# The last 64 rows of a down-projection: two full-height products per bank replaced by three half-height products on the two halves of TensorE's rows

## The chip, the cores and the metric

The kernel is one layer of a hybrid decoder (attention part, gated MLP, final norm) in float32 for 2048 tokens of width 1024. It runs on one core of a Trainium2 chip. The metric is the device time of one execution in microseconds (us). Three runs of the kernel before gave 3138.59, 3139.66 and 3145.38 us; the median is 3139.66 us.

## The reference, cut to what matters

Only the very end of the layer is touched: the down-projection of the gated MLP, the gated residual add and the final norm.

```python
D_MODEL = 1024; SEQ = 2048
D_FF = int(round(8 * D_MODEL / 3 / 64)) * 64        # 2752 = 21 * 128 + 64
...
    u = causal_depthwise_conv(h @ w_up[l], conv_w[l], conv_b[l])
    u_gate, u_val = jnp.split(u, 2, axis=-1)
    x = x + gate_m * ((jax.nn.silu(u_gate) * u_val) @ w_down[l])
return rms_norm(x, g_final)
```

The contraction runs over 2752 rows of `w_down`, which is 21 blocks of 128 and one of 64.

## The kernel before, in words

Matrix products are made in TensorE's one-pass float32 type. To keep float32 precision every operand is held in two parts, high and low: `split` (line 43) rounds the operand on ScalarE (line 44, `hi`), and another engine subtracts that from the operand (line 45, `lo`). A product of two such operands is then three products into the same bank of PSUM, high by high, high by low and low by high; low by low is left out.

The down-projection (lines 926 to 993) runs over four blocks of 512 tokens (`tb`). A block has eight banks of PSUM, four groups `t` of 128 tokens by two halves `n` of the 1024 output columns. In the names of the profile the banks of `t` = 0 and 1 are `ps_o`, those of `t` = 2 are `ps_t`, those of `t` = 3 are `ps_bc`. For each block `k` of contraction rows, `load` (line 928) brings 128 rows of `w_down` (`wdraw`) and of the activations (`graw`) from DRAM and splits them into `wd` and `g`: ScalarE makes both high parts, VectorE the low part of `wd`, GpSimd the low part of `g`. The buffers of `wd` and `g` are six each. `step` (line 957) issues the three products of one `k`, one `t` and one `n`. Each has a weight load of 128x128 from `g` and streams 512 columns of `wd`.

For `k` = 0 to 17 the products of all eight banks are issued `k` by `k` (lines 964 to 971). The last four, `k` = 18 to 21, are kept in `tail` and issued bank by bank (lines 972 to 981), so that a bank is finished, multiplied by the gate (line 983), added to the residual (line 984) and squared (line 986) while TensorE goes on with the next one. After both halves of a group `t`, its norm is made (lines 987 to 989) and the result scaled and written out (lines 992 and 993).

The block `k` = 21 has 64 rows only, and is loaded twice, to partitions 0 to 63 and 64 to 127. In `wd` both copies are split alike. In `g` the upper copy is the high part (line 941) and the lower copy is replaced by the low part (line 942), so that one product over 128 rows gives high plus low of the activations by one part of the weights. Two such products, with `wd` high and `wd` low, make this block: two for each bank, four for each `t`. This also adds low by low, at no further instruction.

The kernel is written in straight code and a scheduler sets the order in which each engine's instructions stand, from the code and from its own estimate of times; the engines wait for one another by semaphores, each engine in its own order. A line elsewhere is of use below: the transposes of line 537 take four blocks of 43 rows through TensorE, in the attention part. The built program gives every product a tile of TensorE's rows and columns. Nearly all have the full 128x128 at row 0; these four have 64x128 at row 0.

Of the kernel before, what the change touches and what calls it, by code (L numbers as in the profile page):

```python
# [11 lines left out]
AF = mybir.ActivationFunctionType  # L12
# [4 lines left out]
P = 128  # L17
# [6 lines left out]
TB = 512  # L24
NTB = S // TB
DFF = 2752
NFULL = DFF // P
REST = DFF - NFULL * P
# [5 lines left out]
def kernel(ctx: ExitStack, tc: tile.TileContext, x, c, w_ada, b_ada, g_attn, w_in, b_fgate,  # L34
                      g_out_fox, g_out_sb, w_out, g_mlp, w_up, conv_w, conv_b, w_down, g_final, out):
    nc = tc.nc
# [3 lines left out]
    def f(t):  # L40
        return t.bitcast(F32)

    def split(hi, lo, src, lo_engine=None):
        nc.scalar.activation(hi, src, AF.Copy)  # L44
        (lo_engine or nc.gpsimd).tensor_sub(lo, src, f(hi))  # L45
# [52 lines left out]
    def modulate(pool, pst, xts, mod, dest, done, tag, lo_engine=None, affine_dve=False, junk=None, prepare=None):  # L98
        n = len(xts) * P
        step = 1 if prepare else len(xts)  # L100
        for j in range(0, len(xts), step):
            r = rms_scale(pool, xts[j:j + step], tag, junk)
            for i, xt in enumerate(xts[j:j + step]):
                nc.vector.tensor_scalar_mul(xt, xt, r[:, i:i + 1])
        yield
        hs_ = []
        for kt in range(KT):
            if prepare:
                prepare(kt)
            ps = pst()  # L110
            for i, xt in enumerate(xts):
                nc.tensor.transpose(ps[:, i * P:(i + 1) * P], xt[:, kt * P:(kt + 1) * P], ident)
            hf = pool.tile([P, n], F32, name=f"hf_{tag}", bufs=2)
            if affine_dve:
                nc.vector.tensor_scalar(hf, ps[:, :n], mod[:, 0, kt:kt + 1], mod[:, 1, kt:kt + 1], ALU.mult, ALU.add)
            else:
                nc.scalar.activation(hf, ps[:, :n], AF.Identity, scale=mod[:, 0, kt:kt + 1], bias=mod[:, 1, kt:kt + 1])
            h = dest(kt)
            split(h[:, 0], h[:, 1], hf, lo_engine)
            hs_.append(h)  # L120
            if kt:
                done(kt - 1, hs_[kt - 1])
            yield
        done(KT - 1, hs_[-1])
        yield
# [36 lines left out]
    def bank(pool, tag, bufs):  # L162
        return pool.tile([P, 512], F32, name=f"ps_{tag}", tag=tag, bufs=bufs)
# [20 lines left out]
    b = pv()  # L184
# [65 lines left out]
    def load_w(kind, p):  # L250
        base = (0 if kind == "fox" else 3 * 512) + p * P
        lo_engine = nc.vector if kind == "sb" else None

        def load(tag, kt, first, step):
            raw = sl_.tile([P, 2, P], F32, name=f"raw_{tag}", tag="wraw", bufs=3)
            nc.sync.dma_start(raw, w_in[kt * P:(kt + 1) * P, first:first + (step + 1) * P].rearrange(
                "p (a n) -> p a n", n=P)[:, 0:step + 1:step, :])
            n = 2 * P + (NH if tag == "v" else 0)
            w_ = sl_.tile([P, 2, n], F32R, name=f"w_{tag}", bufs=8)
            w = w_[:, :, 0:2 * P].rearrange("p s (a n) -> p s a n", n=P)  # L260
            split(w[:, 0], w[:, 1], raw, lo_engine)
            if tag == "v" and (kind, p) == ("sb", 0):
                split(w_[:, 0, 2 * P:], w_[:, 1, 2 * P:], wfr[:, kt], nc.vector)
            return w if tag == "qk" else w_

        def load_qk(kt):
            qk_.append(load("qk", kt, base, 4))

        def load_v():
            return [load("v", kt, base + 1024, 1) for kt in range(KT)] if p % 2 == 0 else None  # L270

        qk_ = []
        if (kind, p) == ("sb", 0):
            return [qk_, load_qk, load_v]
        for kt in range(KT):
            load_qk(kt)
        return [qk_, load_v()]
# [381 lines left out]
    for i, u in enumerate(units):  # L659
# [14 lines left out]
        if kind == "fox":  # L674
            n = sum(2 * (2 + 2 * tb + j2 + 1) for j2 in range(2)) + 1
        else:
            n = sum(2 * (tb + 1 + 2 * tb + j2 + 1) for j2 in range(2)) + 1
# [64 lines left out]
    def bank_a():  # L742
        return bank(psd, "o", 4)
# [139 lines left out]
    for sblk in range(2):  # L883
# [21 lines left out]
        a, b = bank_a(), bank_a()  # L905
# [22 lines left out]
    def load(k, tb):  # L928
        n = P if k < NFULL else REST
        g = dp.tile([P, 2, TB], F32R, name="g", bufs=6)  # L930
        wraw = dp.tile([P, D], F32, name="wdraw", bufs=3)
        graw = dp.tile([P, TB], F32, name="graw", bufs=2)
        w = dp.tile([P, 2, D], F32R, name="wd", bufs=6)
        for r in range(P // n):
            nc.sync.dma_start(wraw[r * n:(r + 1) * n], w_down[k * P:k * P + n, :])
            nc.sync.dma_start(graw[r * n:(r + 1) * n], gs[k][tb // 2][:, tb % 2 * TB:(tb % 2 + 1) * TB])
        split(w[:, 0], w[:, 1], wraw, nc.vector)
        if n == P:
            split(g[:, 0], g[:, 1], graw)
        else:  # L940
            nc.scalar.activation(g[:, 0], graw, AF.Copy)
            nc.vector.tensor_sub(g[REST:P, 0], graw[REST:P], f(g[REST:P, 0]))
        return g, w

    de = open_pool("end")
# [3 lines left out]
    NKD = NFULL + 1  # L949
    for tb in range(NTB):  # L950
        if tb == 0:
            nc.sync.dma_start(gm, gate_m)
            nc.sync.dma_start(gf, g_final.rearrange("(o n) -> o n", o=1).to_broadcast([P, D]))
        banks = [[bank(psd, "o", 4) for _ in range(2)] for _ in range(2)]
        banks += [[bank(psd, "t", 2) for _ in range(2)], [bank(psc, "bc", 2) for _ in range(2)]]

        def step(k, g, w, t, n):
            seq = ((0, 0), (0, 1), (1, 0)) if k < NFULL else ((0, 0), (0, 1))
            for i, (a, b) in enumerate(seq):
                nc.tensor.matmul(banks[t][n], g[:, a, t * P:(t + 1) * P], w[:, b, n * TB:(n + 1) * TB],  # L960
                                 start=k == 0 and i == 0, stop=k == NKD - 1 and i == len(seq) - 1)

        tail = []
        for k in range(NKD):
            g, w = load(k, tb)
            if k >= NKD - LAST:
                tail.append((k, g, w))
                continue
            for t in range(4):
                for n in range(2):  # L970
                    step(k, g, w, t, n)
        for t in range(4):
            row = tb * 4 + t
            xt = de.tile([P, D], F32, name="xo", bufs=4)
            nc.sync.dma_start(xt, x1s[row])
            ss = de.tile([P, 2], F32, name="sl_f", bufs=4)
            r = de.tile([P, 1], F32, name="r_f", bufs=4)
            for n in range(2):
                sl = slice(n * TB, (n + 1) * TB)
                for k, g, w in tail:  # L980
                    step(k, g, w, t, n)
                y = de.tile([P, TB], F32, name="yo", bufs=4)
                nc.vector.tensor_mul(y, banks[t][n], gm[:, sl])
                nc.vector.tensor_add(xt[:, sl], xt[:, sl], y)
                junk = de.tile([P, TB], BF16, name="junk_f", bufs=2)
                nc.scalar.activation(junk, xt[:, sl], AF.Square, accum_out=ss[:, n:n + 1])
            nc.vector.tensor_add(r, ss[:, 0:1], ss[:, 1:2])
            nc.scalar.activation(r, r, AF.Sqrt, bias=epsc, scale=1.0 / D)
            nc.vector.reciprocal(r, r)
            for n, q in enumerate((nc.sync, nc.scalar)):  # L990
                sl = slice(n * TB, (n + 1) * TB)
                nc.vector.scalar_tensor_tensor(xt[:, sl], xt[:, sl], r, gf[:, sl], ALU.mult, ALU.mult)
                q.dma_start(out[row * P:(row + 1) * P, sl], xt[:, sl])
# [27 lines left out]
```

## Time and profile before

| | |
|---|---|
| median of three runs | 3139.66 us |
| the profiled execution's own time | 3141.04 us |
| its span, first to last instruction | 3139.3 us |
| mean granted TensorE clock over the span | 0.983 |
| TensorE busy with products / with weight loads | 95% / 80% of the span |
| VectorE / ScalarE / GpSimd busy | 68% / 54% / 39% |
| first down-projection product starts | 2657.3 us |
| products of the down-projection (line 960) | 2080 |

The profile is of one execution. The time outside its span is 1.7 us. In the views a row of PE is a product, a row of PEld a weight load; a row with xN merges N instructions of a kind that follow one another, from the start of the first to the end of the last. Ends of products are modelled and overlap the next product, so distances between starts tell the rate.

### The profile page before, as it was taken

How to read it: one execution, taken by the hardware profiler on the slowest of the kernel's cores; microseconds unless marked ns; L12 is line 12 of the kernel's file. 1: busy time of each engine (PE TensorE's matmuls, PEld its weight loads, DVE VectorE, ACT ScalarE, POOL GpSimd, SP SyncE). 2: the span in 40 equal slices, each digit the busy share in tenths (PEclk: the TensorE clock that was granted, in tenths of full speed). 3: DMA queues.
4: the chain of work that ended last, by engine and by line, in shares of the span. 5: the costliest groups of instructions: out<-in, count | busy, mean ns of one | idle time of the engine just before them, and what ended most of it. 6: DMA issues, size and time to landing. Idle time of an engine off the chain costs nothing. (4 is left out here: it accounts for less than half of the span.)

```text
span 3139.3 us, 46425 instructions
## 1 busy us (share of the span) xinstructions
PE 2967.0 (95%) x15934; PEld 2511.6 (80%) x15934; DVE 2145.5 (68%) x3342; ACT 1691.0 (54%) x3161; POOL 1227.1 (39%) x1387
## 2 busy tenths in 40 slices
PE   6889998989989999999999999999899998999998
PEld 5778787877878889888877678888678887888887
DVE  6787888878875876556843587778987776354253
ACT  5666776666756676567744444444444444343332
POOL 1554455456553242242212344344444442322321
PEclk8999999999999999999999999999999999999999
DMA  9547542555336696585446632222222223554552
GB/s 267 177 140 255 168 136 69 182 185 155 123 108 221 214 314 211 158 313 162 164 158 222 212 97 86 86 83 83 82 82 89 85 81 130 190 199 161 189 199 90
DMA packets 292940, 496.51 MB, mean 158 GB/s; under 512 B 29448, under 2 KB 177664, under 8 KB 291680
## 3 DMA queue, kind: packets, MB, share of 16 engines
q1 hardware_dynamic: 281072, 480.92, 47.9%
q10 hardware_dynamic: 11632, 12.63, 1.1%
q8 instruction: 126, 2.06, 0.3%
q14 instruction: 110, 0.90, 0.1%
HBM read 352.61 MB, written 90.51 MB: 141 GB/s over the span
## 5 line engine op out<-in xcount | busy, mean ns | idle before, releaser
L810 PE MATMUL ps_o<-oa,wu 128*128 128x512 f32 x2088 | 503.5, 392 | 14.4 <-DVE oa L45 6.9
L810 PEld LDWEIGHTS ps_o<-oa,wu 128*128 128x128 f32 x2088 | 390.5, 188 | 105.5 <-DVE oa L45 10.7
L397 PE MATMUL ps_pv<-at,V 128*128 128x256 f32 x2304 | 410.9, 296 | 41.6 <-DVE at L393 24.8
L393 DVE TENSOR_TENSOR at<-ps_pt,at 128x512 fp32r<-128x512 f32 (+1 forms) x576 | 366.0, 653 | 102.8 <-ACT at L392 99.8
L281 PE MATMUL ps_pj<-hp,w_qk 128*128 128x512 f32 x1512 | 418.4, 406 | 11.1 <-ACT hp L44 3.1
L420 POOL TENSOR_TENSOR a<-a,r 128x512 f32<-128x512 f32 (+3 forms) x240 | 283.4, 1182 | 368.8 <-DVE r L416 112.3
L392 ACT ACTIVATE at<-ps_pt 128x512 fp32r<-128x512 f32 (+1 forms) x576 | 319.4, 577 | 179.8 <-PE ps_pt L388 147.3
L397 PEld LDWEIGHTS ps_pv<-at,V 128*128 128x128 f32 x2304 | 337.0, 192 | 84.6 <-DVE at L393 42.8
L281 PEld LDWEIGHTS ps_pj<-hp,w_qk 128*128 128x128 f32 x1512 | 275.7, 191 | 65.4 <-POOL hp L45 4.0
L45 DVE TENSOR_TENSOR wd<-wdraw,wd 128x1024 fp32r<-128x1024 f32 x88 | 112.4, 1277 | 261.4 <-ACT wd L44 261.4
L378 PE MATMUL ps_qk<-K,Q 128*128 128x512 f32 (+2 forms) x640 | 264.1, 414 | 11.3 <-DMA K<-q 5.8
L419 DVE TENSOR_TENSOR_SCAN r<-r 128x513 f32<-128x513 f32 x192 | 258.0, 1355 | 21.7 <-ACT r L410 14.5
L45 POOL TENSOR_TENSOR g<-graw,g 128x512 fp32r<-128x512 f32 x84 | 141.3, 1684 | 326.8 <-ACT g L44 326.8
L960 PE MATMUL ps_o<-wd,g 128*128 128x512 f32 x1040 | 250.8, 391 | 8.8 <-ACT g L44 8.8
L810 PE MATMUL ps_t<-ob,wu 128*128 128x512 f32 x984 | 243.2, 392 | 0.0
L320 PE MATMUL ps_pj<-w_v,hp 128*128 128x256 f32 (+1 forms) x1536 | 234.1, 291 | 4.8 <-DVE q L45 2.2
L379 PE MATMUL ps_qk<-K,Q 128*128 128x512 f32 (+2 forms) x640 | 238.1, 373 | 0.0
L960 PEld LDWEIGHTS ps_o<-wd,g 128*128 128x128 f32 x1040 | 196.2, 189 | 50.0 <-ACT g L44 9.2
L44 ACT ACTIVATE wu<-wuraw 128x512 fp32r<-128x512 f32 x214 | 133.2, 626 | 185.5 <-PE ps_o L810 111.5
L320 PEld LDWEIGHTS ps_pj<-w_v,hp 128*128 128x128 f32 x1536 | 211.8, 193 | 15.5 <-DVE q L45 3.1
L810 PEld LDWEIGHTS ps_t<-ob,wu 128*128 128x128 f32 x984 | 186.2, 189 | 39.4 <-DVE wu L45 0.3
L388 PE MATMUL ps_pt<-edge,a 128*128 128x128 f32 x1088 | 187.3, 281 | 27.6 <-POOL a L420 14.7
(217 smaller groups left out, 5743.3 us busy)
## 6 DMA issues: line engine op xcount, KB each, us to landing
hp<-hs SPq DMA_DIRECT2D x224, 512.0 KB
wuraw<-in_w_up_dram SPq DMA_DIRECT2D x84, 512.0 KB
wdraw<-in_w_down_dram SPq DMA_DIRECT2D x84, 512.0 KB
Q<-q SPq DMA_DIRECT2D x128, 256.0 KB
g<-u SPq DMA_DIRECT2D x42, 512.0 KB
graw<-g SPq DMA_DIRECT2D x84, 256.0 KB
hs<-hp SPq DMA_DIRECT2D x32, 512.0 KB
K<-q SPq DMA_DIRECT2D x128, 128.0 KB
```

What stands on the lines that cost most here:

```text
L45: (lo_engine or nc.gpsimd).tensor_sub(lo, src, f(hi))
L281: nc.tensor.matmul(acc, w[kt][:, a, n], h[:, bb], start=kt == 0 and i == 0, stop=kt == KT - 1 and i == 2)
L320: nc.tensor.matmul(av[:, t * width:(t + 1) * width], hts[kt][:, a, tok], w[1][kt][:, bb, 0:width], start=kt == 0 and m == 0, stop=kt == KT ...
L378: nc.tensor.matmul(b[:, :cw], Q[:, hl, 0, qcols], K[:, hl, :cw], start=True, stop=False)
L379: nc.tensor.matmul(b[:, :cw], Q[:, hl, 1, qcols], K[:, hl, :cw], start=False, stop=True)
L392: nc.scalar.activation(at[:, 0, lo:], b[:, lo:], AF.Copy)
L393: nc.vector.tensor_sub(at[:, 1, lo:], b[:, lo:], f(at[:, 0, lo:]))
L397: nc.tensor.matmul(o[:, 0:2 * P], V[kt // 4][:, kt % 4, hl, :], rhs, start=first and kk == 0 and w == 0, stop=last and kk == 1 and w == 1)
L419: nc.vector.tensor_tensor_scan(rev, rev, rev, 1.0, ALU.mult, ALU.bypass)
L420: (nc.vector if (ch + qi) % 4 == 0 else nc.gpsimd).tensor_mul(a[:, :need], a[:, :need], r[:, 1:need + 1])
L810: nc.tensor.matmul(b, w[:, p, j], o[:, q], start=first and i == 0, stop=last and i == 2, skip_group_check=True)
L960: nc.tensor.matmul(banks[t][n], g[:, a, t * P:(t + 1) * P], w[:, b, n * TB:(n + 1) * TB], start=k == 0 and i == 0, stop=k == NKD - 1 and i ...
```

## The change

The 64-row block is taken out of `tail`. Its activations are now split as all others are: both copies of `g` get a high and a low part, the low part on GpSimd. A new function, `step_rest`, issues the three products high by high, high by low and low by high for each half `n` of the columns with a contraction of 64 rows: for `n` = 0 from partitions 0 to 63 and for `n` = 1 from partitions 64 to 127, in turns. It is called once for each `t`, ahead of the products of `k` = 18 to 20, and starts or stops no bank.

```diff
             nc.sync.dma_start(graw[r * n:(r + 1) * n], gs[k][tb // 2][:, tb % 2 * TB:(tb % 2 + 1) * TB])
         split(w[:, 0], w[:, 1], wraw, nc.vector)
-        if n == P:
-            split(g[:, 0], g[:, 1], graw)
-        else:
-            nc.scalar.activation(g[:, 0], graw, AF.Copy)
-            nc.vector.tensor_sub(g[REST:P, 0], graw[REST:P], f(g[REST:P, 0]))
+        split(g[:, 0], g[:, 1], graw)
         return g, w
...
         def step(k, g, w, t, n):
-            seq = ((0, 0), (0, 1), (1, 0)) if k < NFULL else ((0, 0), (0, 1))
-            for i, (a, b) in enumerate(seq):
+            for i, (a, b) in enumerate(((0, 0), (0, 1), (1, 0))):
                 nc.tensor.matmul(banks[t][n], g[:, a, t * P:(t + 1) * P], w[:, b, n * TB:(n + 1) * TB],
-                                 start=k == 0 and i == 0, stop=k == NKD - 1 and i == len(seq) - 1)
+                                 start=k == 0 and i == 0, stop=k == NFULL - 1 and i == 2)
+
+        def step_rest(g, w, t):
+
+            for a, b in ((0, 0), (0, 1), (1, 0)):
+                for n in range(2):
+                    r = slice(n * REST, (n + 1) * REST)
+                    nc.tensor.matmul(banks[t][n], g[r, a, t * P:(t + 1) * P], w[r, b, n * TB:(n + 1) * TB],
+                                     start=False, stop=False)
 
         tail = []
         for k in range(NKD):
             g, w = load(k, tb)
+            if k == NFULL:
+                rest = g, w
+                continue
             if k >= NKD - LAST:
...
             r = de.tile([P, 1], F32, name="r_f", bufs=4)
+            step_rest(*rest, t)
             for n in range(2):
```

The built program gives the products of `step_rest` tiles of 64x128, at row 0 for `n` = 0 and at row 64 for `n` = 1. Up to the down-projection every engine's instructions stand as before.

On TensorE the products stand as follows at the end of the last block of tokens, before the change. The last three rows are the tail: eleven products for each of the eight banks.

```order
L960 MATMUL ps_o<-wd,g 128x512 x12
L960 MATMUL ps_t<-wd,g 128x512 x6
L960 MATMUL ps_bc<-wd,g 128x512 x6
L960 MATMUL ps_o<-wd,g 128x512 x44
L960 MATMUL ps_t<-wd,g 128x512 x22
L960 MATMUL ps_bc<-wd,g 128x512 x22
```

At the same place after the change (line 955 is `step`, line 963 `step_rest`; the size is that of the output) this stands.

```order
L955 MATMUL ps_o<-wd,g 128x512 x12
L955 MATMUL ps_t<-wd,g 128x512 x6
L955 MATMUL ps_bc<-wd,g 128x512 x6
L963 MATMUL ps_o<-wd,g 128x512 x6
L955 MATMUL ps_o<-wd,g 128x512 x18
L963 MATMUL ps_o<-wd,g 128x512 x6
L955 MATMUL ps_o<-wd,g 128x512 x18
L963 MATMUL ps_t<-wd,g 128x512 x6
L955 MATMUL ps_t<-wd,g 128x512 x18
L963 MATMUL ps_bc<-wd,g 128x512 x6
L955 MATMUL ps_bc<-wd,g 128x512 x18
```

Each group `t` now begins with six products of half height, and the bank of its first half is finished nine products before that of its second half, where it was eleven.

On VectorE the program's last instructions stand so before: `yo` is a bank times the gate, `xo` the residual row, `r_f` the norm.

```order
L983 TENSOR_TENSOR yo<-ps_bc,gm 128x512
L987 TENSOR_TENSOR r_f<-sl_f 128x1
L984 TENSOR_TENSOR xo<-xo,yo 128x512
L989 RECIPROCAL r_f<-r_f 128x1
L992 SCALAR_TENSOR_TENSOR xo<-xo,r_f,gf 128x512 x2
L983 TENSOR_TENSOR yo<-ps_bc,gm 128x512
L984 TENSOR_TENSOR xo<-xo,yo 128x512
L987 TENSOR_TENSOR r_f<-sl_f 128x1
L989 RECIPROCAL r_f<-r_f 128x1
L992 SCALAR_TENSOR_TENSOR xo<-xo,r_f,gf 128x512 x2
```

After the change they stand so.

```order
L994 TENSOR_TENSOR r_f<-sl_f 128x1
L990 TENSOR_TENSOR yo<-ps_bc,gm 128x512
L996 RECIPROCAL r_f<-r_f 128x1
L991 TENSOR_TENSOR xo<-xo,yo 128x512
L999 SCALAR_TENSOR_TENSOR xo<-xo,r_f,gf 128x512 x2
L990 TENSOR_TENSOR yo<-ps_bc,gm 128x512
L991 TENSOR_TENSOR xo<-xo,yo 128x512
L994 TENSOR_TENSOR r_f<-sl_f 128x1
L996 RECIPROCAL r_f<-r_f 128x1
L999 SCALAR_TENSOR_TENSOR xo<-xo,r_f,gf 128x512 x2
```

Only the sum of the norm of `t` = 2 has moved, ahead of the first half's multiplication; the two scalings of `t` = 2 still stand between the two halves of `t` = 3.

## Rows read from the trace of the kernel before

**Rows 1.** The page: busy us of each engine, share of the span, instructions.
```profile
PE 2967.0 (95%) x15934; PEld 2511.6 (80%) x15934; DVE 2145.5 (68%) x3342; ACT 1691.0 (54%) x3161; POOL 1227.1 (39%) x1387
```

**Rows 2.** Busy us by stretch (PE, PEld, DVE, ACT, POOL), granted clock, DMA share, GB/s.
```profile
2774.00:2891.00 117.00, 117.00 (x518) 96.89 (x517) 47.65 (x55) 41.32 (x64) 35.59 (x21) 1.00 0.55 184
2891.00:3009.00 118.00, 118.00 (x522) 97.69 (x522) 48.53 (x57) 41.32 (x64) 35.30 (x21) 1.00 0.55 183
...
3111.15:3131.10 19.95, 19.95 (x89) 16.33 (x87) 13.43 (x26) 5.95 (x17) 0.00 (x0) 1.00 0.15 54
```

**Rows 3.** Waits, 2656 to 3140 us: us in total, times, longest.
```profile
POOL g L45 <- ACT g L44: 326.8, 81, 26.9
...
ACT wd L44 <- PE ps_bc L960: 196.8, 58, 3.9
...
PE ps_o L960 <- ACT g L44: 8.8, 1, 8.8
```

**Rows 4.** Chain that ended last, its last bank: start us, us, what.
```profile
3126.27 2.51 PE ps_bc L960 x11
...
3128.80 0.16 DVE yo L983
...
3130.33 1.42 DVE xo L992 x2
3131.74 0.61 DVE yo L983
```

**Rows 5.** TensorE's timeline, tail of the first block: start us, us, merged instructions.
```profile
2757.55 10.14 PE L960 MATMUL ps_o<-wd,g 128*128 128x512 f32 x44
2767.52 5.15 PE L960 MATMUL ps_t<-wd,g 128*128 128x512 f32 x22
...
2777.50 2.88 PE L960 MATMUL ps_o<-wd,g 128*128 128x512 f32 x12
...
2788.38 2.88 PE L960 MATMUL ps_o<-wd,g 128*128 128x512 f32 x12
```

**Rows 6.** TensorE's timeline in the attention part, around line 537.
```profile
946.40 0.39 PE L379 MATMUL ps_qk<-K,Q 128*128 128x512 f32 x1
946.63 0.60 PE L388 MATMUL ps_pt<-edge,p 128*128 128x128 f32 x4
947.16 0.44 PE L537 MATMUL ps_pt<-edge,hp 43*128 43x43 f32 x4
947.53 0.38 PE L378 MATMUL ps_qk<-K,Q 128*128 128x256 f32 x1
947.75 0.28 PE L379 MATMUL ps_qk<-K,Q 128*128 128x256 f32 x1
```

**Rows 7.** The same place in narrower stretches: products from 946.955, then from 947.36 us.
```profile
946.74 0.49 PE L388 MATMUL ps_pt<-edge,p 128*128 128x128 f32 x3
...
947.87 0.40 PE L281 MATMUL ps_pj<-hp,w_qk 128*128 128x512 f32 x1
```

**Rows 8.** All engines there, the loads and the VectorE work ahead of them.
```profile
946.54 0.16 DVE L490 SCALAR_TENSOR_TENSOR ls<-ls 128x4 f32<-128x4 f32 x1
...
947.16 0.32 PEld L537 LDWEIGHTS ps_pt<-edge,hp 43*128 43x128 f32 x4 [0.17 <-issue]
...
947.53 0.19 PEld L378 LDWEIGHTS ps_qk<-K,Q 128*128 128x128 f32 x1
```

**Rows 9.** Line 537's products: duration ns min/median/max.
```profile
L537 PE MATMUL ps_pt<-edge,hp x4: 232/232/253, 947.2 to 947.4; 43*128 43x43 f32 x4
```

**Rows 10.** All engines while the 64-row block of the first token block is split.
```profile
2747.84 0.61 ACT L941 ACTIVATE g<-graw 128x512 fp32r<-128x512 f32 x1
...
2749.22 0.69 DVE L942 TENSOR_TENSOR g<-graw,g 64x512 fp32r<-64x512 f32 x1
...
2753.97 1.80 POOL L45 TENSOR_TENSOR g<-graw,g 128x512 fp32r<-128x512 f32 x1 [9.07 <-ACT g L44]
```

**Rows 11.** ScalarE, where the next block takes over the tail's buffers.
```profile
2775.88 1.06 ACT L44 ACTIVATE wd<-wdraw 128x1024 fp32r<-128x1024 f32 x1 [0.58 <-PE ps_bc L960]
```

## The prediction, made before the change was run

> **What bounds the kernel now.** I read the page first: TensorE is busy for 95% of the span [rows 1], which says nothing yet about the stage that is changed. So I read busy time by stretch. In the two middle token blocks of the down-projection TensorE's busy time equals the stretch, 117.00 of 117.00 and 118.00 of 118.00 us, at a granted clock of 1.00, which is the 2.4 GHz level; the other four engines are busy for less than half of it [rows 2]. The list of waits agrees: in the whole stage TensorE waits once, 8.8 us at its very start, while GpSimd and ScalarE spend their time waiting for others [rows 3]. The chain that ended last runs through TensorE's products until 3128.78 us and leaves it only for the last bank's eviction [rows 4]. So a product taken out of this stage, or added, counts in full, and the price of one is the distance of starts: 9.97 us for 44 [rows 5], 0.2267 us. The recorded durations are longer and mean nothing here.
>
> The last 10.5 us deserve a look of their own. The second half of the last group is done on TensorE at about 3131.3 us (22 products after 3126.27), but its multiplication by the gate starts late, because VectorE is still scaling the rows of the group before: the chain goes from the first half's bank (11 products) by way of VectorE [rows 4]. The end hangs on when the *first* half of the last group is finished.
>
> **What goes.** 16 groups (four blocks, four `t`) lose four full-height products each: 4 × 0.2267 = 0.907 us a group. The subtraction on VectorE, 0.69 us in each block [rows 10], goes too; VectorE is not late in mid-stage, so that is worth nothing.
>
> **What comes, off the path.** GpSimd gets four subtractions of 1.80 us [rows 10], one a block. GpSimd is busy for 35 of 118 us [rows 2]. The high part of the block was written from 2747.84 us on; 0.61 and 1.80 us later, at about 2750.3, the low part can be there, and the tail starts at 2757.55 [rows 5]: over 7 us of cover. That the 64-row block is now used first in the tail and not last eats 2.0 us (9 products) which are not needed. If the cover were gone, a wait of up to 1.8 us a block would stand on TensorE, 7 us in all. The tail's buffers of `k` = 18 to 20 come free two products later in relation to the block's end (0.45 us). ScalarE now refills the first of them at 2775.88 [rows 11], and TensorE needs it only two steps into the next block, at 2788.38 [rows 5]: 11 us of cover, no cost.
>
> **What comes, on the path.** Each group gets six products over 64 rows, three pairs of an upper and a lower one.
>
> *The pairs.* No row shows two products on different halves of TensorE's rows. The bounds are full overlap, where a pair takes as long as one product, 3 × 0.227 = 0.68 us, and none, 6 × 0.227 = 1.36 us. I take full overlap. The nearest row for it is that of line 537, where the array is run as tiles of 64 rows: four products start 0.07 us apart ((0.44 − 0.23) / 3) although each lasts 0.23 us [rows 6, 9]. So in that mode several products are under way at once and the loads run ahead of them. The lower product must start after the upper one; after the last pair this lag stays: between 0 and 0.11 us (a full-height start, rows 6); I take 0.06, near line 537's distance.
>
> The Trainium skill (TensorE: Matmul & The Clock Gate, Part 3, measured speedup) says that products on different row groups run together, with starts some 4 ns apart, and gives 3.07 times for four of 32 rows. By that the lag would be nil and the sum below smaller by 1 us; no run here shows it yet.
>
> *Going into the 64-row mode.* The four transposes of line 388 ahead of line 537 start 0.11 us apart (946.63, 946.74), so the last starts at 946.96 [rows 6, 7]. The first load of line 537 starts 0.20 us later, at 947.16, together with its product, and its idle time is put down to "issue": nothing that it waited for; the last VectorE instruction that had ended by then did so 0.46 us before, at 946.70 [rows 8]. That is 0.09 us over the usual 0.11. Besides, the load is no longer hidden behind a running product. Between 0.02 us (longest against median product of line 537, rows 9) and 0.10 us (below); I take 0.10, since the new loads are of the same kind as those below and not transposes. Sum 0.19; lower bound 0, if the drain belongs to transposes alone.
>
> *Coming out of it.* The last product of line 537 starts at 947.16 + 0.44 − 0.23 = 947.37; the next load and product, full height again, start at 947.53, 0.16 later where 0.07 was the rule: 0.09 [rows 6, 8]. That product then lasts 0.38 us where its twin lasts 0.28, and the twin starts 0.22 us after it, where the next distance is 0.12 [rows 6, 7]: 0.10 us for a load that nothing hides. Sum 0.19; lower bound again 0.
>
> The Trainium skill has a rule that speaks against this change (TensorEngine Tiling (Array Packing), key properties): tiles run in parallel, but changing the tiling mode, not merely the tile, drains TensorE. The trace agrees, at 0.09 us each way plus a bare load; without that rule the sum would be the gain of the last rival below.
>
> *The sum.* A group: 0.19 + 0.68 + 0.06 + 0.19 − 0.91 = +0.21 us. Sixteen groups: +3.4 us.
>
> *The end.* The first half of the last group is now finished after the six and nine more products, and only nine follow it where eleven did. VectorE's work between the two halves is as long as before (3128.80 to 3131.74 us, rows 4), so the last eviction falls 2 × 0.227 = 0.45 us further behind TensorE: +0.4 us. Bounds: nothing, if VectorE keeps up, to 0.5.
>
> In total +3.8 us: the profiled execution's 3141.04 us would become 3144.8; that execution was 1.4 us above the median of the runs, 3139.66, so I predict 3139.66 + 3.8 = **3143.5 us**. By the bounds above it ends between 3141.2 (bare first load 0.02, no lag) and 3144.4 (lag 0.11).
>
> **The rivals.**
>
> *No overlap* (slower, the other side). If the lower product starts only when the upper one is through, a group takes 0.19 + 1.36 + 0.19 − 0.91 = +0.83 us, sixteen 13.3, with the end 13.8: 3153.4 us. For it: no row shows overlap of two halves. Against: the split of the array that rows 6 show by their drains would then serve nothing, and line 537's products overlap one another. It decides against the kernel as soon as a pair takes longer than about 0.29 us: 0.38 + 3 × 0.29 + 0.06 − 0.91 = +0.4, sixteen 6.4 us, which is 0.2%.
>
> *Overlap, but bare loads.* If the loads of one half don't run ahead while the other half works, each pair takes 0.227 + 0.10 = 0.33 us: a group 0.09 + 0.99 + 0.06 + 0.19 − 0.91 = +0.42, in total 6.7 + 0.4 = +7.1: 3146.8 us. Against it: line 537's loads do run ahead.
>
> *Free switching* (a small gain). If the drains of line 537 come from its being a transpose, or are covered behind products of 512 columns, a group takes 0.68 + 0.06 − 0.91 = −0.17, in total −2.7 + 0.4 = −2.3: 3137.4 us; at the very best 3136.5 (no lag, 16 × −0.227 = −3.6, end +0.4). For it: there is only one place in the trace to read the price from. Against: the row names no cause but issue, and the full-height transposes of line 388 follow a product without a break, 946.63 after 946.40 [rows 6].
>
> **How the numbers follow.** A difference under 0.2%, 6.3 us, is about what a measurement of this kernel can't tell from no change. Chances: mode switches at line 537's price with overlap 0.50 (3143.5, within 0.2%); free switching 0.18 (3137.4, within); bare loads 0.15 (3146.8, slower by 0.23%); no overlap 0.15 (3153.4, slower by 0.44%); something else 0.02. The range 3136.3 to 3149.5 us takes the first three with their bounds and leaves out no overlap: some 0.8. Faster by over 0.2% would need 3133.4 or less; not even sixteen groups at the full saving of a product reach that: 0.02. Slower by over 0.2% are both slow rivals, 0.30; within 0.2% the rest, 0.68.
>
> **What would show each step right or wrong.** In TensorE's timeline the six products of line 963: starts in three pairs, 0.23 us from pair to pair and under 0.11 us inside one, show the overlap; six starts 0.23 us apart refute it; pairs at 0.33 us show the bare loads. The first load of line 963 should start about 0.09 us later than a load does in the rows ahead of it, and the first product of line 955 after it should come about 0.19 us late. The four tails should last 20.8 us where they last 19.95. TensorE should still wait for nothing between the blocks; a wait for GpSimd's `g` at the start of a tail would make the cover wrong. At the end VectorE's last multiplication by the gate should start some 0.8 us after TensorE's last product, where it is 0.4 now. A time below 3138 or above 3146 us would make the likeliest case wrong.

## The result and the profile after

| | before | after |
|---|---|---|
| median, 19 runs each | 3141.97 us | 3145.91 us |
| lowest to highest | 3134.51 to 3145.38 us | 3141.61 to 3153.76 us |
| the profiled execution, its span | 3141.04, 3139.3 us | 3147.76, 3145.4 us |
| first down-projection product starts | 2657.32 us | 2659.82 us |
| from it to the last product's start | 473.55 us | 476.89 us |
| a later block, first start to the next block's first start | 117.87 us | 118.71 us |
| the last product's start to the end of the span | 8.39 us | 8.66 us |

The ratio of the times is 1.0017, with a 95% interval of 1.0010 to 1.0024, so the change costs 3.1 to 7.5 us. That is a small loss. At 0.17% it lies inside the 0.2% that the prediction called no change (the interval's upper end, 0.24%, does not), and its 3143.5 us (+3.8) was near. The two profiled executions lie 6.7 us apart, but only 3.3 us of it is in the stage (476.89 − 473.55) and 0.3 us in the end. Of the rest, 2.5 us lie ahead of the first down-projection product, where no engine's instructions differ, and 0.6 us outside the span (3147.76 − 3145.4 against 3141.04 − 3139.3). In the profiles of all the kernels of this study that product starts between 2654.76 and 2659.82 us, in no relation to what was changed. So the length of the stage is what to read here, not the total. One run of all those below was slow (e4, 4158.92 us at a mean granted clock of 0.654); it is left out of e4's median and ratio.

The page says as little as it did before; it answers to [rows 1].

```profile
PE 2972.9 (95%) x15966; PEld 2506.0 (80%) x15966; DVE 2141.3 (68%) x3338; ACT 1690.8 (54%) x3161; POOL 1233.1 (39%) x1391
```

The windows from the first product of a block to that of the next are sharper. The columns are those of [rows 2]: length, then busy time of PE, PEld, DVE, ACT and POOL, granted clock, DMA share, GB/s. First one block of before, then two of after.

```profile
2777.50:2895.36 117.86, 117.86 (x521) 97.60 (x520) 48.48 (x56) 41.32 (x65) 35.59 (x21) 1.00 0.56 185
```

```profile
2780.82:2899.52 118.70, 118.70 (x529) 96.25 (x528) 48.07 (x56) 41.48 (x65) 38.06 (x23) 1.00 0.56 184
...
2899.52:3018.23 118.71, 118.71 (x529) 96.25 (x528) 46.20 (x55) 41.47 (x65) 37.69 (x22) 1.00 0.53 181
```

TensorE is still busy for the whole stretch at a granted clock of 1.00, the 2.4 GHz level. A block has grown by 0.84 us, 0.21 us for each of its four groups. Eight more products stand in a block (528 where 520 stood; a window counts one or two more at its edges), while the time of the weight loads has fallen, since the loads of a pair now lie beside one another.

TensorE's timeline of the first block's tail answers to [rows 5].

```profile
2760.12 0.97 PE L963 MATMUL ps_o<-wd,g 64*128 64x512 f32 x6
2761.02 4.37 PE L955 MATMUL ps_o<-wd,g 128*128 128x512 f32 x18
...
2775.72 0.96 PE L963 MATMUL ps_bc<-wd,g 64*128 64x512 f32 x6
2776.61 4.37 PE L955 MATMUL ps_bc<-wd,g 128*128 128x512 f32 x18
2780.82 2.88 PE L955 MATMUL ps_o<-wd,g 128*128 128x512 f32 x12
```

The four tails last 2780.82 − 2760.12 = 20.70 us where they lasted 19.95. Six half-height products of a group take 0.90 us from their first start to the start of the next full one; six full ones would take 1.36.

Inside one group, in narrow stretches of the same timeline (a row is cut where the stretch ends, so its start and its count are what to read):

```profile
2765.00 0.39 PE L955 MATMUL ps_o<-wd,g 128*128 128x512 f32 x1
2765.32 0.50 PE L963 MATMUL ps_o<-wd,g 64*128 64x512 f32 x2
...
2765.66 0.63 PE L963 MATMUL ps_o<-wd,g 64*128 64x512 f32 x4
...
2765.89 0.39 PE L963 MATMUL ps_o<-wd,g 64*128 64x512 f32 x2
2766.22 0.50 PE L955 MATMUL ps_o<-wd,g 128*128 128x512 f32 x1
```

The half-height products come in pairs, at 2765.32, 2765.66 and 2765.89; in the trace's ns the two of a pair start 3 to 4 ns apart here (2 to 4 over all groups). The steps between starts are 0.32 (full to first pair), 0.33, 0.23, 0.32 (last pair to full) us, where 0.227 is the rule; the second full product follows after another 0.33. So there are four slow steps in a group, two on the way in and two on the way out. The weight loads show what is different there (TensorE's loads; in brackets the idle time before and what ended it):

```profile
2765.32 0.53 PEld L963 LDWEIGHTS ps_o<-wd,g 64*128 64x128 f32 x6 [0.35 <-issue]
2766.21 3.95 PEld L955 LDWEIGHTS ps_o<-wd,g 128*128 128x128 f32 x18 [0.37 <-issue]
```

Elsewhere a load starts well ahead of its product, at 2764.78 for the one that starts at 2765.00. At either switch it starts with its own product, 1 to 2 ns ahead of it in the trace's ns, after an idle time that nothing in the profile accounts for but "issue", as at line 537 in [rows 8]. All groups of line 963 show it, 16 times:

```profile
L963 PE MATMUL ps_o<-wd,g x48: 386/393/493, 2760.1 to 3122.0; 64*128 64x512 f32 x48
...
  issue: 5.6, 16
```

The longest of its products, 493 ns, are those whose load was bare, that is, not hidden behind a running product.

### The profile page after: what moved, and what is told of

Read it like the earlier page. It is cut to its first block, busy times and chain, and to the rows that moved or that the text cites. A ratio compares the mean times of both kernels' runs of the same rounds, so it can differ in the third digit from the quotient of the medians.

```text
span 3145.4 us, 46491 instructions
## 1 busy us (share of the span) xinstructions
PE 2972.9 (95%) x15966; PEld 2506.0 (80%) x15966; DVE 2141.3 (68%) x3338; ACT 1690.8 (54%) x3161; POOL 1233.1 (39%) x1391
## 5 line engine op out<-in xcount | busy, mean ns | idle before, releaser
L45 POOL TENSOR_TENSOR g<-graw,g 128x512 fp32r<-128x512 f32 x88 | 150.9, 1715 | 325.0 <-ACT g L44 321.3
L955 PEld LDWEIGHTS ps_o<-wd,g 128*128 128x128 f32 x1008 | 189.6, 189 | 51.1 <-ACT g L44 9.1
L44 ACT ACTIVATE wd<-wdraw 128x1024 fp32r<-128x1024 f32 x88 | 93.1, 1058 | 230.4 <-PE ps_bc L955 201.7
```

## The experiments

All of them keep everything ahead of the down-projection, and each ratio is to runs of the kernel before on the same chip (medians 3140.83 us for e1 to e4, 3141.53 us for e5 to e7, so the medians in the table are not to be divided by its first row). What decides is a later block, from its first product's start to the first of the next. Those starts are taken from the traces in ns; the window rows below show the same lengths.

| kernel | a block, us | stage, us | median, us | ratio to before, 95% |
|---|---|---|---|---|
| before | 117.87 | 473.55 | 3141.97 | |
| after | 118.71 | 476.89 | 3145.91 | 1.0017, 1.0010 to 1.0024 |
| e1_order_only | 117.87 | 473.25 | 3141.52 | 1.0005, 0.9996 to 1.0014 |
| e2_same_half | 121.47 | 488.62 | 3156.71 | 1.0048, 1.0034 to 1.0061 |
| e3_not_in_turns | 118.73 | 477.17 | 3144.66 | 1.0007, 0.9997 to 1.0017 |
| e4_once_per_block | 117.45 | 471.72 | 3142.44 | 1.0001, 0.9991 to 1.0010 |
| e5_three_entries | 122.27 | 491.25 | 3161.78 | 1.0065, 1.0049 to 1.0080 |
| e6_upper_only | 118.69 | 476.83 | 3147.85, one run | |
| e7_96_rows | 119.89 | 481.36 | 3150.40 | 1.0030, 1.0016 to 1.0043 |

### e1: only the new place in the order

From before: the 64-row block leaves the tail and stands ahead of each group, as in the changed kernel, but with its two products over 128 rows a bank, and the old split of `g`.

```diff
+        def step_rest(g, w, t):
+            for b in range(2):
+                for n in range(2):
+                    nc.tensor.matmul(banks[t][n], g[:, 0, t * P:(t + 1) * P], w[:, b, n * TB:(n + 1) * TB],
+                                     start=False, stop=False)
...
+            step_rest(*rest, t)
             for n in range(2):
```

> The 64-row block is used at the head of each group as in the changed kernel, but still as two full-height products per bank. The measure is the distance from the first to the last product start of the down-projection, 473.55 us before and 476.89 us after the change. Theory (TensorE pays for going into and out of the 64-row mode, the order costs nothing but at the very end): 473.5 to 473.7 us, and the time from the last product's start to the end 8.6 to 8.8 us, where it was 8.39 before and 8.66 after; in total within 1 us of before. Rival (the new place of the block costs, by a wait or by buffers): about 476.9 us as after the change.

One block, and VectorE at the end of the program:

```profile
2779.21:2897.08 117.87, 117.87 (x522) 97.60 (x520) 46.89 (x56) 41.54 (x65) 35.92 (x21) 1.00 0.53 182
```

```profile
3130.97 0.69 DVE L992 TENSOR_TENSOR yo<-ps_bc,gm 128x512 f32<-128x512 f32 x1 [0.72 <-PE ps_bc L959]
3131.58 0.15 DVE L996 TENSOR_TENSOR r_f<-sl_f 128x1 f32<-128x1 f32 x1
...
3133.83 0.68 DVE L992 TENSOR_TENSOR yo<-ps_bc,gm 128x512 f32<-128x512 f32 x1
```

The block is as long as before. The new place costs the stage nothing, neither by a block that is needed earlier nor by buffers that come free later, so the stage's loss in the changed kernel is not in the order. (The stage's 473.25 us lies under the expected 473.5 because its first block, with the wait at the start, took 119.88 us in place of 120.18. The new split on GpSimd is not in e1; it is looked at further down.) At the end VectorE's two multiplications by the gate stand 2.86 us apart, with the sum of line 996 between them. From the last product's start to the end it is 8.85 us where before has 8.39: 0.46 us more, the prediction's end term, and a little over the 8.6 to 8.8 us expected for this run.

### e2: both halves of the columns on the upper rows

From after. The same products of the same size, with no second half of the rows to run on.

```diff
-                    r = slice(n * REST, (n + 1) * REST)
+                    r = slice(0, REST)
```

> All six products of the 64-row block use partitions 0 to 63, so both halves of the columns take the upper half of TensorE's rows; the result is the same, since both copies are. Theory (pairs overlap, and only because the two are on different halves): six starts 0.227 us apart, each group longer by 3 x 0.227 = 0.68 us, first to last product start 476.9 + 10.9 = 487.8 us, in total 10.9 us over the changed kernel. Rival (the pairs' starts of 3 ns in the trace don't mean that both stream at once, the work is serial anyway): 476.9 us, as after the change.

One block, and two rows of TensorE's timeline in the first tail:

```profile
2783.67:2905.13 121.46, 121.46 (x529) 98.43 (x528) 46.90 (x55) 41.42 (x65) 38.07 (x22) 1.00 0.53 178
```

```profile
2777.87 1.66 PE L963 MATMUL ps_bc<-wd,g 64*128 64x512 f32 x6
2779.46 4.37 PE L955 MATMUL ps_bc<-wd,g 128*128 128x512 f32 x18
```

Now the six products of a group reach over 1.59 us (2777.87 to 2779.46) where they took 0.90. A block is 121.47 − 118.71 = 2.76 us longer, 0.69 us a group, which is three products at 0.23. In the trace's ns no two of the six start less than 224 ns apart. So in the changed kernel the two halves run together, and the overlap is worth three products a group. The rival "no overlap" is out.

### e3: three upper products, then three lower ones

From after. The loops change places, so that TensorE is given upper, upper, upper, lower, lower, lower.

```diff
-            for a, b in ((0, 0), (0, 1), (1, 0)):
-                for n in range(2):
+            for n in range(2):
+                for a, b in ((0, 0), (0, 1), (1, 0)):
```

> The upper half's three products come first, then the lower half's three. Theory (products start strictly in their order, so that a lower one can overlap only the last upper one): five steps of 0.227 us in place of three, each group longer by 0.45 us, first to last product start 476.9 + 7.3 = 484.2 us. Rival (each half works off its own products, the turns don't matter): 476.9 us.

One block, and the first group of the first tail in narrow stretches of TensorE's timeline:

```profile
2775.96:2894.69 118.73, 118.73 (x530) 96.31 (x528) 47.71 (x56) 41.46 (x65) 38.46 (x23) 1.00 0.54 184
```

```profile
2754.91 0.39 PE L955 MATMUL ps_bc<-wd,g 128*128 128x512 f32 x1
2755.23 0.50 PE L963 MATMUL ps_o<-wd,g 64*128 64x512 f32 x2
...
2755.23 0.97 PE L963 MATMUL ps_o<-wd,g 64*128 64x512 f32 x6
2756.14 0.96 PE L955 MATMUL ps_o<-wd,g 128*128 128x512 f32 x3
```

Two products start at 2755.23, and the next full one 0.90 us after the first of the six, as in turns. A block is 0.03 us longer. The built program does give the six as upper, upper, upper, lower, lower, lower, and a row doesn't name its half; but two products on one half never start this close (e2), so each pair is an upper and a lower one. My theory, that TensorE starts products strictly in the program's order and that the lower ones would wait for the third upper one, fell. In the trace's ns the pairs start at 2755.233 and .243, 2755.568 and .578, 2755.803 and .813. Each half of the rows works off its own products, and the lower one starts 10 ns behind the upper, about three times the 2 to 4 ns that it lags when it is given second; here it is given fourth. "In turns" is not what makes the overlap.

### e4: all the half-height products of a block at one place

From after. The four groups' products are issued together ahead of the first tail, so a block has one way in and one way out where it had four of each.

```diff
+        for t in range(4):
+            step_rest(*rest, t)
...
-            step_rest(*rest, t)
```

> All 24 half-height products of a token block are issued in one go ahead of its tail, so that the 64-row mode is entered and left 4 times in place of 16. Theory (0.39 us for an entry and an exit, 12 overlapped pairs in place of 16 full products): each block 0.39 + 12 x 0.227 - 16 x 0.227 = -0.52 us against before, first to last product start 473.55 - 2.1 = 471.5 us, with 0.3 us lost at the end in total 1.8 us under before and 5.4 us under the changed kernel. Rival (the place of the block or something outside the stage costs the time, not the switches): 476 us or more.

One block, and TensorE's timeline of the first tail:

```profile
2778.82:2896.27 117.45, 117.45 (x530) 96.69 (x528) 46.88 (x55) 41.42 (x65) 39.99 (x22) 1.00 0.55 183
```

```profile
2759.37 1.66 PE L963 MATMUL ps_o<-wd,g 64*128 64x512 f32 x12
2760.87 0.86 PE L963 MATMUL ps_t<-wd,g 64*128 64x512 f32 x6
2761.57 0.84 PE L963 MATMUL ps_bc<-wd,g 64*128 64x512 f32 x6
2762.34 8.48 PE L955 MATMUL ps_o<-wd,g 128*128 128x512 f32 x36
```

Twelve pairs pass in 2.97 us (2759.37 to 2762.34). A block is 1.25 us shorter than the changed kernel's: three switches in and out saved, 0.42 us each. It is also 0.41 us shorter than before's, and the stage 1.83 us. The total shows none of it: the ratio is 1.0001, with an interval wider than the gain, the end takes 0.45 us back (8.84 where before has 8.39), and the time outside the span, further down, 0.6 us more. It is the best of the half-height forms, and it beats the kernel before only in its stage.

### e5: three ways in a group

From after. The three pairs of a group are issued one by one, ahead of the three full steps of the tail.

```diff
-            step_rest(*rest, t)
...
-                for k, g, w in tail:
+                for j, (k, g, w) in enumerate(tail):
+                    if n == 0:
+                        step_rest(*rest, t, (((0, 0), (0, 1), (1, 0))[j],))
```

> The three pairs of a group are issued one by one, each ahead of one of the three full-height steps of the first half, so that the 64-row mode is entered and left 48 times in place of 16. Nothing else is added. The measure is the distance from the first to the last product start within one of the three later token blocks, 117.64 us before and 118.48 after the change. Theory (each entry and exit costs 0.39 to 0.41 us): 8 more a block, 118.48 + 3.1 to 3.3 = 121.6 to 121.8 us, and the total 12.5 to 13.1 us over the changed kernel. Rival (the price is of the half-height products themselves, not of the switches): 118.5 us.

One block, and one group in TensorE's timeline:

```profile
2783.92:2906.19 122.27, 122.27 (x529) 95.89 (x528) 47.98 (x55) 41.65 (x65) 37.77 (x23) 1.00 0.53 176
```

```profile
2777.93 0.50 PE L963 MATMUL ps_bc<-wd,g 64*128 64x512 f32 x2
2778.36 0.97 PE L955 MATMUL ps_bc<-wd,g 128*128 128x512 f32 x3
2779.26 0.50 PE L963 MATMUL ps_bc<-wd,g 64*128 64x512 f32 x2
2779.69 0.98 PE L955 MATMUL ps_bc<-wd,g 128*128 128x512 f32 x3
```

A block is 122.27 − 118.71 = 3.56 us longer, for eight more ways in and out: 0.445 us each, somewhat more than expected. The price of a switch, and not of a group as such, is what the changed kernel pays.

### e6: the lower half's products left out

From after.

```diff
-                for n in range(2):
+                for n in range(1):
```

> The lower half's three products are left out, so the second half of the output's columns lacks the last 64 rows of the contraction. Theory (the lower products run beside the upper ones and cost only their lag of 3 ns): a later block takes 118.48 us as with them, within 0.05. Rival (the two halves share the stream of columns or the writing to PSUM, each product costs time of its own): down to 118.48 - 4 x 0.68 = 115.8 us.

One block, and a group in TensorE's timeline:

```profile
2780.77:2899.46 118.69, 118.69 (x518) 96.22 (x516) 47.09 (x55) 41.64 (x65) 37.31 (x22) 1.00 0.55 182
```

```profile
2775.66 0.96 PE L963 MATMUL ps_bc<-wd,g 64*128 64x512 f32 x3
2776.56 4.37 PE L955 MATMUL ps_bc<-wd,g 128*128 128x512 f32 x18
```

Three products alone take 0.96 us and the next full one starts 0.90 us after the first, as with six. The lower half's twelve products of a block cost 118.707 − 118.693 = 0.014 us. They are hidden whole.

### e7: six products over 96 rows

From after. Both halves of the columns use partitions 0 to 95, more than half of the rows.

```diff
-                    r = slice(n * REST, (n + 1) * REST)
+                    r = slice(0, 96)
```

> The six products of a group take partitions 0 to 95 for both halves of the columns, so 32 rows of the contraction are counted twice and the output isn't the reference's. The built program gives such products the full 128x128 tile, so there is no change of mode and no overlap. Theory (the switches cost because of the 64-row tile): two full-rate products more than before in each group, 117.64 + 4 x 2 x 0.2267 = 119.45 us for a later block, under the 121.24 us of the same six products on 64 rows by 4 x 0.45 us, and starts 0.227 us apart without a longer one on the way in or out. Rival (any product over fewer than 128 rows stops the pipeline): 121.2 us.

One block, and the way in of one group in TensorE's timeline:

```profile
2777.10:2897.00 119.90, 119.90 (x530) 99.13 (x528) 46.21 (x55) 41.42 (x65) 37.41 (x22) 1.00 0.54 181
```

```profile
2771.61 1.55 PE L963 MATMUL ps_bc<-wd,g 96*128 96x512 f32 x6
2773.00 4.27 PE L955 MATMUL ps_bc<-wd,g 128*128 128x512 f32 x18
```

The six reach over 1.39 us (2771.61 to 2773.00) where e2's six over 64 rows reach over 1.59, and no step going in or out is long: in the trace's ns all of them are 226 to 237, and the first of the six loads starts at 2771.39, 0.22 us ahead of its product. A block is 1.57 us shorter than e2's, 0.39 us a group. So the switch price belongs to the 64-row tile, not to products that use fewer rows than the ones before them. Here 0.05 us a group stays above the usual 0.227 a product (119.893 − 117.866 − 8 × 0.2267 = 0.21 us a block), and that without a bare load: the products from the first of the six on start 0.226 to 0.237 us apart for a while.

## Why the prediction was right, point by point

**The bound.** TensorE's products set the stage: it is busy all of each block, and the waits from 2656 to 3150 us have only the one at the start, as [rows 3].

```profile
POOL g L45 <- ACT g L44: 321.3, 85, 26.8
...
PE ps_o L955 <- ACT g L44: 8.7, 1, 8.7
```

**Off the path.** GpSimd's new subtraction is done at 2752.81 us and the tail starts at 2760.12: 7.3 us of cover, where the prediction had over 7.

```profile
2751.01 1.80 POOL L45 TENSOR_TENSOR g<-graw,g 128x512 fp32r<-128x512 f32 x1 [3.64 <-ACT g L44]
```

With the waits above that shows the new split to cost nothing; for the later buffers e1's block of unchanged length does.

**The pairs.** Predicted 0.68 us and a lag of 0.06. The overlap is full (e2, e6). The lag was mis-sized: it is 2 to 4 ns, not 60. I had taken line 537's distance of starts for it, but products of that line stand on one half of the rows. Nor did that line support the overlap itself: it has one half only, full-height products, too, start closer (0.227 us) than their records last (0.39 us), and e2's six on one half start one by one. So full overlap was the right choice between the two bounds, but not for the reason given. The Trainium skill (TensorE: Matmul & The Clock Gate, Part 3, measured speedup) has starts some 4 ns apart, and the trace agrees with it.

**Going in and coming out.** Predicted 0.19 us each, 0.09 for the drain and 0.10 for a bare load, from the four products of line 537. In the trace's ns the groups of the changed kernel show 318 and 332 on the way in, and 320 and 334 or 323 and 338 in turn on the way out, against 227: 0.196 us, and 0.200 or 0.207 us (mean 0.204). The first step of each two is 0.09 to 0.10 us too long, in the prediction the drain; the second 0.10 to 0.11, in the prediction the bare load. The other measures of one way in and out are 0.39 (e7 against e2), 0.42 (e4) and 0.445 us (e5); predicted was 0.38. The rule cited from the Trainium skill (TensorEngine Tiling (Array Packing), key properties), that a change of the tiling mode drains TensorE, agrees: e7, which keeps the full tile, has no such step.

**The sum of a group.** Predicted +0.21 us, measured 118.707 − 117.866 = 0.841 us for four, +0.21. That the two agree is partly luck: misses cancel. The 0.06 of lag isn't there. Instead 0.68 + 0.196 + 0.204 − 0.907 = 0.17 leaves 0.04 us to steps of 0.228 to 0.236 around the switches, which the prediction didn't have. e7 has such steps without a switch and without a bare load, so neither is needed for them; their cause stays open. Sixteen groups: +3.3 us measured (476.89 − 473.55), +3.4 predicted.

**The end.** Predicted +0.45 us, measured 8.66 − 8.39 = +0.27. The chain of the changed kernel, from the last group's first half on, answers to [rows 4]:

```profile
3132.80 2.28 PE ps_bc L955 x9
...
3135.10 0.28 DVE yo L990
...
3136.51 1.32 DVE xo L999 x2
3137.84 0.61 DVE yo L990
```

The path is the one foretold, nine products and then VectorE. The step that failed is "VectorE's work between the two halves is as long as before". Its rows there now read:

```profile
3134.82 0.16 DVE L994 TENSOR_TENSOR r_f<-sl_f 128x1 f32<-128x1 f32 x1 [0.85 <-ACT junk_f L993]
3135.10 0.69 DVE L990 TENSOR_TENSOR yo<-ps_bc,gm 128x512 f32<-128x512 f32 x1
...
3137.76 0.69 DVE L990 TENSOR_TENSOR yo<-ps_bc,gm 128x512 f32<-128x512 f32 x1
```

The sum of the norm stands ahead of the first half's multiplication, as the order told before the run, and the two multiplications are 2.66 us apart instead of 2.86 (before, and e1, where the sum stands between them). That 0.2 us is the miss. Before, they stood so:

```profile
3128.80 0.69 DVE L983 TENSOR_TENSOR yo<-ps_bc,gm 128x512 f32<-128x512 f32 x1 [0.72 <-PE ps_bc L960]
...
3131.66 0.68 DVE L983 TENSOR_TENSOR yo<-ps_bc,gm 128x512 f32<-128x512 f32 x1
```

The last multiplication starts 0.66 us after the last product ends at 3137.10, where 0.8 was foretold and 0.4 was before.

**The rivals.** No overlap would have given a block as e2's, 121.47 us. Bare loads would have put the pairs 0.33 us apart; only the first step between pairs is that, the second is 0.23, and that first one is the bare load of the entry. Free switching would have made a block shorter than before, 117.2 us by its −0.17 a group; it is 118.71. So the case that came is the likeliest one, with its own mechanism.

**The total.** +3.8 us was predicted; the stage and the end grew by 3.6 us, and the medians of 19 runs lie 3.9 us apart. The prediction has no term for the time outside the span, but that has grown: it is 2.35 to 2.47 us in all 19 runs after the change, 1.73 to 1.91 in the 36 runs of before that stand beside the experiments. That is 0.6 us more; e1 doesn't have it (1.74 to 1.91), so it isn't the new order, and no run here tells what it is. The parts then add up to +4.2 us, inside the interval of 3.1 to 7.5, and that the forecast's +3.8 is so near owes something to misses on both sides. 3145.91 us itself lies above the 3141.2 to 3144.4 that the prediction gave for its likeliest case, and 0.1 us under the 3146 above which that case was to be called wrong. That it stands 2.4 us over the predicted 3143.5 comes nearly all from the base: the three runs that were known had a median of 3139.66, all nineteen have 3141.97.

## What to carry to other kernels

Two products over 64 rows on different halves of TensorE's rows cost one here, in either order of issue that was run; but each visit to that mode cost 0.39 to 0.45 us here, as much as two full products of 512 columns (0.227 each). Count the products saved per visit, not per kernel: one saved per visit lost 0.21 us, four saved in one visit (e4) won 0.41. And where a change is worth a few us of a time that scatters by ten, read the length of its stage from first start to first start, which here repeats to 0.01 us.

## What was not expected of the hardware

- Products for the lower half of the rows that stand behind three for the upper half don't wait for these: pairs start 10 ns apart in e3, 2 to 4 ns apart in turns.
- The drain needs the 64-row tile. Going from 128 to 96 rows and back cost no step longer than 0.237 us (e7).
- After a change of the row count, with the 64-row tile or with 96 rows, products start up to 0.24 us apart (0.237 in e7, 0.241 in e5) where 0.227 is the rule, for some products on end. No run here tells why.
- The time outside the span grew by 0.6 us with the changed kernel and not with e1. No run here tells why.
